# A hybrid decoder step on one Trainium2 core: one more stream step ahead of two transposes, a key multiply in two parts, other mixing rates

## The chip, the core and the metric

The kernel runs on one core of one Trainium2 chip. The metric is the device time of one execution in microseconds (us). The kernel before takes 1997.62 us (median of 3 runs, 1997.28 to 1998.98). A difference of 0.2% is about 4 us.

## The reference, cut to what matters

One layer is computed for a prompt of 1024 tokens and for 8 running sequences of 8 new tokens each (64 "sample" tokens), width 1024, all in float32:

```python
x = x + 0.5 * rms_norm(swiglu(rms_norm(x, norm_ffn1_pre), ffn1_w_gu, ffn1_w_down), norm_ffn1_post)
h = rms_norm(x, norm_mix_pre)
z = h @ w_in + b_in                    # 2816 columns: q, k, v | hq, hf, hi, hg
a = rms_norm(window_attention(q, k, v, attn_sinks), attn_out_norm)   # 8 heads of 64, 2 key heads, window 128
f = lb + (1 - lb) * sigmoid(hf)
o, S = hgrn2_chunked(silu(hq), 1 - f, log(f), hi, s0)                # 4 heads, state 128 x 128
o = rms_norm(o, hg_out_norm) * silu(hg)
x = x + rms_norm(concat([a, o]) @ w_out, norm_mix_post)
x = x + 0.5 * rms_norm(swiglu(rms_norm(x, norm_ffn2_pre), ffn2_w_gu, ffn2_w_down), norm_ffn2_post)
```

Beside the new `x` it returns the last window of keys and values and the recurrent state, for prompt and samples.

## The kernel before

The 1088 tokens are three groups: group 0 has two blocks of 128 prompt tokens and the 64 sample tokens (320 columns), groups 1 and 2 have three blocks of 128 each (384 columns). Every weight matrix is split into a high and a low part (`split`, lines 257 to 259: a cast on ScalarE, then a difference on VectorE), and a product is three matmuls (`mm3`, lines 279 to 281). The rest of the work is fitted between these products.

That is done with streams. A stream is a Python generator with a rate. The code that writes out the big products calls `tick()` at fixed places; each tick adds the rate to a stream's account, and for each whole unit the generator runs to its next `yield`. So a `yield` is a step boundary: what stands behind it is written out at least one step later, with products between. `need(name)` runs a stream to its end at once. What is written out is then ordered engine by engine by a planner that works with its own costs, so the order of the program is that of the ticks only in the large.

The middle of the kernel, the mixing stage (some 690 to 1345 us of the profiled span), goes so: the input projection `w_in_units(0)`, then stream `m0` (the mixer of group 0, rate `RM[0]`) beside the last second-half pieces of the first feed-forward and `w_in_units(1)`; `need("m0")`, then `m1` (rate `RM[1]`) beside `w_out_units(0)`, `w_in_units(2)` and the first columns of the second feed-forward (`f2.head`); `need("m1")`, then `m2` (rate `RM[2]`) beside `w_out_units(1)` and more of `f2.head`; `need("m2")`, then `w_out_units(2)`. Streams `c0`, `c1`, `c2` carry the norms and the transposes between the stages at the same time.

A mixer runs two chains of generators in turn, one step of each (`both`). The attention chain has one `attn_block` for each block: for each of two pairs of heads the scores (`sc`, line 1178), the masked maxima (1186) and exponentials (1195), two yields, the transposes of the probabilities (`pT`, 1206), a yield, the product with the values (`pv`, 1219), a yield; then `finish_attn` (square, `rsqrt`, scale, a yield, the transposes `oT` at 1154, and `put_mix`, which stores the high and the low part). The recurrence chain begins with `intra`: for seven distances `h` of 1 to 64 it multiplies the query half of each block on VectorE (1297) and the key half on GpSimd (1299), between small products (`lv` at 1258; `l32` and `l64` at 1289). Then comes one `hgrn_block` for each block: the key's transposes `kT` (1335), the outputs `av` (1341, 1344), the state's update `u` (1348), and `finish_hgrn` (squares, `rsqrt`, scale at 1314, a yield, the transposes `hT` at 1318, the gate at 1320, `put_mix`). Group 0 also has `sample_attn`, `sample_hgrn` and `kv_out`. The stream of group 1's feed-forward input (`post_n`, `pre_s`: x-loads at line 427, 439, squares at 394, a store to DRAM at 399, in-place scales at 491 and 493, transposes at 511) runs beside `m2`.

Of the kernel before, what the change touches and what calls it, by code (L numbers as in the profile page):

```python
# [14 lines left out]
ALU = mybir.AluOpType  # L15
# [3 lines left out]
P = 128  # L19
# [26 lines left out]
def tile_step(ctx: ExitStack, tc: tile.TileContext, A: dict, O: list):  # L46
    nc = tc.nc
    V, S, G, PE = nc.vector, nc.scalar, nc.gpsimd, nc.tensor
# [8 lines left out]
    def uid(s):  # L57
        cnt[0] += 1
        return f"{s}_{cnt[0]}"
# [4 lines left out]
    def axbank(s="ax"):  # L64
        return ps.tile([P, 512], F32, tag="ax", bufs=4, name=uid(s))
# [31 lines left out]
    def stream(name, gen, rate):  # L97
        streams[name] = [gen, rate, 0.0]
# [155 lines left out]
    def small():  # L254
        return pp.tile([P, 4, 8], F32, tag="small", bufs=10, name=uid("sm"))
# [787 lines left out]
    def mixing(tp, h):  # L1043
        w_in, w_out = A["w_in"][0], A["w_out"][0]

        def t2(shape=(P, 512)):
            return tmp2("t2", shape)
# [90 lines left out]
        def put_mix(n, half, sl, src):  # L1138

            hi, lo = MT[n][0][half], MT[n][1][half]  # L1140
            S.copy(hi[:, :, sl], src)
            V.tensor_tensor(lo[:, :, sl], src, hi[:, :, sl].bitcast(F32), op=ALU.subtract)

        def finish_attn(n, o, r, sl):

            sm = small()
            S.activation(junk[:r], o[:r], AF.Square, accum_out=sm[:r, 0, 0:1])
            V.tensor_scalar(sm[:r, 0, 0:1], sm[:r, 0, 0:1], 1.0 / 512, EPS, op0=ALU.mult, op1=ALU.add)
            rsqrt(sm[:r, 1, 0:1], sm[:r, 0, 0:1], (sm[:r, 2, 0:1], sm[:r, 3, 0:1]))
            V.tensor_scalar(o[:r], o[:r], sm[:r, 1, 0:1], None, op0=ALU.mult)  # L1150
            yield
            b4 = axbank("oT").rearrange("p (c t) -> p c t", c=4)
            for c in range(4):
                PE.transpose(b4[:, c, :r], o[:r, c * P:(c + 1) * P], ident[:r, :r])
            m = t2((P, 4, P))
            V.tensor_tensor(m[:, :, :r], b4[:, :, :r],
                            cols[:, C_AON:C_AON + 4].unsqueeze(2).to_broadcast([P, 4, r]), op=ALU.mult)
            put_mix(n, 0, sl, m[:, :, :r])
            yield
# [70 lines left out]
        def intra(n, res):  # L1230

            z, w, pw = Z[n], WIDTH[n], NPB[n] * P
            K, Q, f = [z[i] for i in ("k", "hq", "f")]
            pool_d = big()
            D = pool_d.rearrange("p a t -> p (a t)")
            At = big(F32, (P, 3, 4, P))
            G.memset(At, 0.0)
            C = tp.tile([P, 3, 4, 32], F32, tag="cm", bufs=1, name=uid("cm"))
            Ds, off = [f[:, :, :w]], 0
            for h in (1, 2, 4, 8, 16, 32, 64):  # L1240
                nx = (w if h <= 4 else pw) // (2 * h)
                Dv = Ds[-1][:, :, :2 * nx].rearrange("p a (x e) -> p a x e", e=2)
                Ds.append(D[:, off:off + 4 * nx].rearrange("p (a x) -> p a x", a=4))
                G.tensor_tensor(Ds[-1], Dv[:, :, :, 0], Dv[:, :, :, 1], op=ALU.mult)
                off += 4 * nx

            def parts(h):

                return [(P, slice(0, 3))] if n else [(P, slice(0, 2))] + ([(NS, slice(2, 3))] if h <= 4 else [])

            def blocks(s, h):
                b5 = axbank(s)[:, :384].rearrange("p (b a t) -> p b a t", b=3, a=4)
                for r, bs in parts(h):
                    for b in range(bs.start, bs.stop):
                        for a in range(4):
                            for i in range(r // 32):
                                cs = slice(b * P + 32 * i, b * P + 32 * i + 32)
                                PE.matmul(b5[32 * i:32 * i + 32, b, a], K[:, a, cs], Q[:, a, cs],  # L1258
                                          start=True, stop=True)
                return b5  # L1260

            b5 = blocks("ld", 1)
            for r, bs in parts(1):
                V.tensor_tensor(C[:r, bs], b5[:r, bs], ident32[:r].unsqueeze(1).unsqueeze(1).to_broadcast(
                    [r, bs.stop - bs.start, 4, 32]), op=ALU.mult)
            V.tensor_tensor(Q[:, :, :w], Q[:, :, :w], f[:, :, :w], op=ALU.mult)
            yield
            for h in reversed(LEVELS):
                if h <= 16:
                    b5 = blocks("lv", h)  # L1270
                    for r, bs in parts(h):
                        nb = 4 * (bs.stop - bs.start)
                        V.copy_predicated(C[:r, bs].rearrange("p b a t -> p (b a) t"),
                                          lmask[h][:r].unsqueeze(1).to_broadcast([r, nb, 32]),
                                          b5[:r, bs].rearrange("p b a t -> p (b a) t"))
                        if (r, h) in ((NS, 4), (P, 16)):
                            for i in range(r // 32):
                                ds = slice(32 * i, 32 * i + 32)
                                G.tensor_copy(At[ds, bs, :, ds], C[ds, bs])
                else:  # L1280
                    per = 3 if h == 32 else 2
                    for b0 in range(0, NPB[n], per):
                        bs = range(b0, min(b0 + per, NPB[n]))
                        b4 = axbank(f"l{h}")[:, :per * 4 * h].rearrange("p (b a t) -> p b a t", b=per, a=4)
                        for b in bs:
                            for a in range(4):
                                for c in range(0, P, 2 * h):
                                    t = b * P + c
                                    PE.matmul(b4[c:c + h, b - b0, a], K[:, a, t:t + h],
                                              Q[:, a, t + h:t + 2 * h], start=True, stop=True)  # L1290
                        for c in range(0, P, 2 * h):
                            S.copy(At[c:c + h, b0:bs[-1] + 1, :, c + h:c + 2 * h], b4[c:c + h, :len(bs)])
                cols = w if h <= 4 else pw
                nx = cols // (2 * h)
                Qv, Kv = [t[:, :, :cols].rearrange("p a (x u) -> p a x u", u=2 * h) for t in (Q, K)]
                Dv = Ds.pop(0)[:, :, :2 * nx].rearrange("p a (x e) -> p a x e", e=2)
                V.tensor_tensor(Qv[:, :, :, h:], Qv[:, :, :, h:], Dv[:, :, :, 0:1].to_broadcast([P, 4, nx, h]),
                                op=ALU.mult)
                G.tensor_tensor(Kv[:, :, :, :h], Kv[:, :, :, :h], Dv[:, :, :, 1:2].to_broadcast([P, 4, nx, h]),
                                op=ALU.mult)  # L1300
                if h == 4:
                    Ds8 = Ds[0]
                yield
            res.update(At=At, Q=Q, K=K, D=Ds[0], D8=Ds8)

        def finish_hgrn(n, bank, r, c0):
            sm = small()
            o = t2((P, 4, P))
            b4 = bank.rearrange("p (a t) -> p a t", a=4)
            for a in range(4):  # L1310
                S.activation(o[:r, a], b4[:r, a], AF.Square, accum_out=sm[:r, 0, a:a + 1])
            V.tensor_scalar(sm[:r, 0, :4], sm[:r, 0, :4], 1.0 / P, EPS, op0=ALU.mult, op1=ALU.add)
            rsqrt(sm[:r, 1, :4], sm[:r, 0, :4], (sm[:r, 2, :4], sm[:r, 3, :4]))
            V.tensor_tensor(o[:r], b4[:r], sm[:r, 1, :4].unsqueeze(2).to_broadcast([r, 4, P]), op=ALU.mult)
            yield
            tb = axbank("hT").rearrange("p (a t) -> p a t", a=4)
            for a in range(4):
                PE.transpose(tb[:, a, :r], o[:r, a], ident[:r, :r])
            m = t2((P, 4, P))
            V.tensor_tensor(m[:, :, :r], tb[:, :, :r], Z[n]["g"][:, :, c0:c0 + r], op=ALU.mult)  # L1320
            put_mix(n, 1, slice(c0, c0 + r), m[:, :, :r])
            yield
# [234 lines left out]
        for g_ in gens:  # L1557
            yield from g_

    RM = [0.95, 1.0, 1.3]  # L1560
    RA0, RA1, RB0, RB1 = 1.2, 0.75, 0.6, 0.8
    HEAD1, HEAD2 = 6, (5, 14, 22)
    PA, PB, PC = (1, 6, 2), (5, 3), (7, 4)
# [8 lines left out]
    xs = [load_x(0, True)]  # L1572
    h = {}
# [65 lines left out]
    with tc.tile_pool(name="mx", bufs=1) as tp:  # L1639
        w_in_units, mixer, w_out_units = mixing(tp, hmix)  # L1640
        need("c0")
        w_in_units(0)
        stream("m0", mixer(0), RM[0])
        half1(1)
# [8 lines left out]
        need("m0")  # L1653
        stream("m1", mixer(1), RM[1])
        w_out_units(0, ym, sums)
# [5 lines left out]
        need("m1")  # L1661
        stream("m2", mixer(2), RM[2])
        w_out_units(1, ym, sums)
# [101 lines left out]
```

## Time and profile before

| | |
|---|---|
| median of 3 runs | 1997.62 us (1997.28 to 1998.98) |
| the profiled execution | 1997.85 us, of which its span is 1996.1 us |
| TensorE matmul busy | 1977.9 us, 99% of the span |
| VectorE, ScalarE, GpSimd busy | 1405.0 us (70%), 942.3 us (47%), 153.1 us (8%) |
| mean granted TensorE clock | 0.995 of full speed |

In the profile PE is TensorE's matmuls, DVE is VectorE, ACT ScalarE, POOL GpSimd, SP the engine that issues most DMAs. A number after L is a line of the kernel. A row of the timeline has start and duration in us, engine, line, operation, output<-input, shape and count, and in brackets the idle time of its engine before it with what ended it. A row of the windows has a stretch in us from the span's start, its length, then for each engine the busy time and the instructions, then PEclk, the granted share of TensorE's clock, then the DMA share and GB/s.

### The profile page before, as it was taken

Reading aid. Unit: us, or ns where it says so; the run is one execution under the profiler, and the core shown is the slowest. Engines: PE = TensorE matmul, PEld = TensorE weight load, DVE = VectorE, ACT = ScalarE, POOL = GpSimd, SP = SyncE. Lnnn points to the kernel's source line nnn. Section 1 sums busy time; section 2 is a strip of 40 time slices with the busy share of each in tenths; the row PEclk is TensorE's granted clock in tenths of the full one; section 3 lists DMA queues with packets and bytes.
Section 4 is the critical chain, followed back from the end, with each engine's and each line's share of the span. In section 5 each row is a group of like instructions: output and inputs, shape, how many; then the busy total and the mean of one; then the engine's idle time right before and its main releaser. Section 6 shows DMA issues by size and latency. Waiting matters only on the chain.

```text
span 1996.1 us, 34286 instructions
## 1 busy us (share of the span) xinstructions
PE 1977.9 (99%) x13331; PEld 1859.0 (93%) x13331; DVE 1405.0 (70%) x2522; ACT 942.3 (47%) x1713; POOL 153.1 (8%) x142
## 2 busy tenths in 40 slices
PE   9999999999999999999999999999999999999998
PEld 9999999999998988779999998989999999999886
DVE  7686767886568656777668656746887887655667
ACT  5753334444445434435344543756544444444452
POOL 0000000000003102210211202000000000000201
PEclk9999999999999999999999999989999999999999
DMA  7735545655777647766334342536565555667874
GB/s 233 221 107 185 189 161 188 227 189 192 234 231 218 183 145 247 233 176 183 108 102 133 95 155 86 171 130 200 165 201 199 191 187 190 211 232 234 287 262 139
DMA packets 377316, 370.28 MB, mean 185 GB/s; under 512 B 40546, under 2 KB 294321, under 8 KB 377137
## 3 DMA queue, kind: packets, MB, share of 16 engines
q1 hardware_dynamic: 371169, 357.21, 56.3%
q10 hardware_dynamic: 5984, 10.88, 1.6%
q8 instruction: 104, 1.70, 0.3%
q14 instruction: 59, 0.48, 0.1%
HBM read 284.31 MB, written 84.71 MB: 185 GB/s over the span
## 4 chain that ended last, share of the span: by engine, by line
PE 96%; DMA 1%; ACT 1%; DVE 1%; issue 0%; POOL 0%; SPq 0%; DVEq 0%; ACTq 0%; POOLq 0%
PE mm L279 28%; PE mm L280 28%; PE mm L281 28%; PE pv L1219 1%; PE sc L1178 1%; PE c L281 1%; PE c L279 1%; PE c L280 1%; DMA raw<-in_ffn_w_gu_dram 1%; PE pT L1206 1%; PE lv L1258 1%; PE tr L511 1%; PE av L1341 0%; PE u L1348 0%; PE av L1344 0%
## 5 line engine op out<-in xcount | busy, mean ns | idle before, releaser
L279 PE MATMUL mm<-h,wsph 128*128 128x320 f32 (+1 forms) x1280 | 406.4, 319 | 0.4 <-ACT sg L676 0.4
L280 PE MATMUL mm<-h,wsph 128*128 128x320 f32 (+1 forms) x1280 | 406.1, 318 | 0.0
L281 PE MATMUL mm<-h,wspl 128*128 128x320 f32 (+1 forms) x1280 | 403.3, 317 | 0.0
L259 DVE TENSOR_TENSOR wspl<-raw,wsph 128x1024 fp32r<-128x1024 f32 x200 | 247.9, 1240 | 151.5 <-ACT wsph L258 145.9
L258 ACT CAST wsph<-raw 128x1024 fp32r<-128x1024 f32 x200 | 209.3, 1048 | 299.1 <-PE mm L280 238.4
L258 ACT CAST w<-raw 128x512 fp32r<-128x512 f32 (+1 forms) x218 | 160.3, 740 | 213.7 <-PE mm L280 113.4
L279 PEld LDWEIGHTS mm<-h,wsph 128*128 128x128 f32 x1280 | 240.7, 188 | 5.5 <-issue 3.8
L259 DVE TENSOR_TENSOR w<-raw,w 128x512 fp32r<-128x512 f32 (+1 forms) x218 | 186.6, 860 | 84.0 <-ACT w L258 83.6
L280 PEld LDWEIGHTS mm<-h,wsph 128*128 128x128 f32 x1280 | 241.0, 188 | 3.1 <-issue 2.7
L281 PEld LDWEIGHTS mm<-h,wspl 128*128 128x128 f32 x1280 | 240.3, 188 | 1.5 <-issue 1.2
L279 PE MATMUL mm<-h,w 128*128 128x384 f32 (+1 forms) x720 | 240.3, 335 | 0.5 <-ACT w L258 0.5
L280 PE MATMUL mm<-h,w 128*128 128x384 f32 (+1 forms) x720 | 240.8, 335 | 0.0
L281 PE MATMUL mm<-h,w 128*128 128x384 f32 (+1 forms) x720 | 235.4, 334 | 0.0
L280 PE MATMUL mm<-w,h 128*128 128x512 f32 x462 | 181.9, 394 | 0.0
L281 PE MATMUL mm<-w,h 128*128 128x512 f32 x462 | 180.3, 392 | 0.0
L279 PE MATMUL mm<-w,h 128*128 128x512 f32 x462 | 180.1, 393 | 0.0
L279 PE MATMUL mm<-big,w 128*128 128x384 f32 x528 | 176.4, 334 | 0.7 <-ACT big L770 0.7
L280 PE MATMUL mm<-big,w 128*128 128x384 f32 x528 | 176.5, 334 | 0.0
L281 PE MATMUL mm<-big,w 128*128 128x384 f32 x528 | 176.2, 334 | 0.0
L279 PEld LDWEIGHTS mm<-h,w 128*128 128x128 f32 x720 | 135.0, 188 | 1.1 <-ACT w L258 0.7
L280 PEld LDWEIGHTS mm<-h,w 128*128 128x128 f32 x720 | 135.2, 188 | 0.1
L281 PEld LDWEIGHTS mm<-h,w 128*128 128x128 f32 x720 | 134.7, 188 | 0.1
(355 smaller groups left out, 3531.3 us busy)
## 6 DMA issues: line engine op xcount, KB each, us to landing
raw<-in_ffn_w_gu_dram SPq DMA_DIRECT2D x156, 512.0 KB
raw<-in_ffn_w_down_dram SPq DMA_DIRECT2D x74, 512.0 KB
raw<-in_w_in_dram SPq DMA_DIRECT2D x54, 512.0 KB
ar<-fa SPq DMA_DIRECT2D x70, 384.0 KB
big<-in_ffn_w_down_dram SPq DMA_DIRECT2D x88, 256.0 KB
fb<-big SPq DMA_DIRECT2D x44, 512.0 KB
fa<-big SPq DMA_DIRECT2D x22, 768.0 KB
raw<-fb SPq DMA_DIRECT2D x30, 512.0 KB
```

The source lines that it names most:

```text
L258: S.copy(hi, src)
L259: (lo_eng or V).tensor_tensor(lo, src, hi.bitcast(F32), op=ALU.subtract)
L279: PE.matmul(out, a[0], b[0], start=first, stop=False, skip_group_check=resume)
L280: PE.matmul(out, a[0], b[1], start=False, stop=False, skip_group_check=resume)
L281: return PE.matmul(out, a[1], b[0], start=False, stop=last, skip_group_check=resume).ins
L511: PE.transpose(bank[:, i * P:(i + 1) * P], y[kh][:, i, k * P:(k + 1) * P], ident)
L1178: PE.matmul(banks[g][:, i * 256:i * 256 + wk], zq[64 * g:64 * g + 64, 2 * pr + i, b * P:(b + 1) * P], kx[64 * g:64 * g + 64, k0:k0 + wk], ...
L1206: PE.transpose(bank[:, (i * nk + kb) * P:(i * nk + kb + 1) * P], pt[g][:, i, kb * P:(kb + 1) * P], ident)
L1219: PE.matmul(ob[:, hd * 64:hd * 64 + 64], pT[g][:, (i * nk + kb) * P:(i * nk + kb + 1) * P], vn[:, vb, g * 64:g * 64 + 64], start=kb == 0, ...
L1258: PE.matmul(b5[32 * i:32 * i + 32, b, a], K[:, a, cs], Q[:, a, cs], start=True, stop=True)
```

## The change

Three edits. (1) `finish_attn` and `finish_hgrn` yield twice, not once, between the scaled result and its transposes. (2) For `h == 64`, GpSimd's multiply of the keys is written as two instructions: the first block, then the other blocks. (3) The rates of the mixers go from 0.95, 1.0, 1.3 to 0.85, 0.95, 1.2.

```diff
@@ finish_attn
             V.tensor_scalar(o[:r], o[:r], sm[:r, 1, 0:1], None, op0=ALU.mult)
+            yield
             yield
             b4 = axbank("oT").rearrange("p (c t) -> p c t", c=4)
@@ intra
-                G.tensor_tensor(Kv[:, :, :, :h], Kv[:, :, :, :h], Dv[:, :, :, 1:2].to_broadcast([P, 4, nx, h]),
-                                op=ALU.mult)
+                for xs in [slice(0, 1), slice(1, nx)] if h == 64 else [slice(0, nx)]:
+                    G.tensor_tensor(Kv[:, :, xs, :h], Kv[:, :, xs, :h],
+                                    Dv[:, :, xs, 1:2].to_broadcast([P, 4, xs.stop - xs.start, h]), op=ALU.mult)
@@ finish_hgrn
             V.tensor_tensor(o[:r], b4[:r], sm[:r, 1, :4].unsqueeze(2).to_broadcast([r, 4, P]), op=ALU.mult)
+            yield
             yield
             tb = axbank("hT").rearrange("p (a t) -> p a t", a=4)
@@
-    RM = [0.95, 1.0, 1.3]
+    RM = [0.85, 0.95, 1.2]
```

## The prediction

> **What bounds the kernel now.** I read the page first, for the engine that has no slack.
>
> ```profile
> span 1996.1 us, 34286 instructions
> ...
> PE 1977.9 (99%) x13331; PEld 1859.0 (93%) x13331; DVE 1405.0 (70%) x2522; ACT 942.3 (47%) x1713; POOL 153.1 (8%) x142
> ```
>
> TensorE is busy for 99% of the span, and the change takes no product away. So it can gain only what TensorE loses: time in which it waits, and time in which it works at a lower clock. The view of waits, for TensorE alone, names the first:
>
> ```profile
> PE pT L1206 <- ACT t L1195: 2.9, 1, 2.9
> PE kT L1335 <- POOL big L1299: 2.4, 1, 2.4
> ...
> PE hT L1318 <- DVE t L1314: 0.9, 1, 0.9
> PE tr L468 <- DVE h L473: 0.9, 1, 0.9
> ...
> PE skT L1379 <- DMA kv<-in_cache_k_win_dram: 0.6, 1, 0.6
> ...
> PE mm L279 <- ACT sg L676: 0.4, 1, 0.4
> ```
>
> All six are in the mixing stage. I then took the stage in stretches of 5 us and kept those in which TensorE is not busy throughout or PEclk is below 1:
>
> ```profile
> 850.00:855.00 5.00, 3.62 (x25) 2.44 (x24) 4.25 (x9) 3.66 (x6) 0.00 (x0) 1.00 0.96 224
> 855.00:860.00 5.00, 4.65 (x22) 3.15 (x22) 2.82 (x5) 1.56 (x2) 0.67 (x1) 1.00 1.21 263
> 1225.00:1230.00 5.00, 2.61 (x34) 2.41 (x34) 2.78 (x3) 0.85 (x2) 2.19 (x1) 1.00 0.38 110
> 1230.00:1235.00 5.00, 5.00 (x29) 5.00 (x28) 2.20 (x11) 4.50 (x12) 0.00 (x0) 0.66 0.00 0
> 1245.00:1250.00 5.00, 4.06 (x31) 3.82 (x30) 3.44 (x13) 3.43 (x11) 0.00 (x0) 1.00 0.35 95
> 1295.00:1300.00 5.00, 2.10 (x12) 1.40 (x10) 1.94 (x5) 4.28 (x10) 0.00 (x0) 0.86 0.54 140
> 1300.00:1305.00 5.00, 5.00 (x19) 3.67 (x17) 1.10 (x2) 4.27 (x9) 0.00 (x0) 0.50 0.19 73
> 1305.00:1310.00 5.00, 5.00 (x16) 3.85 (x16) 1.56 (x8) 0.36 (x1) 0.00 (x0) 0.50 0.10 35
> 1310.00:1315.00 5.00, 5.00 (x32) 4.91 (x31) 1.39 (x6) 2.75 (x10) 0.00 (x0) 0.77 0.00 0
> 1325.00:1330.00 5.00, 4.61 (x33) 4.34 (x32) 1.92 (x2) 2.13 (x5) 0.00 (x0) 1.00 0.65 195
> sum 50.00, PE 41.66 PEld 34.98 DVE 23.39 ACT 27.80 POOL 2.86; mean PE 4.17 PEld 3.50 DVE 2.34 ACT 2.78 POOL 0.29
> ```
>
> Two columns matter. Idle: 50.00 - 41.66 = 8.34 us. Clock: (1 - 0.66) x 5 = 1.70 us behind the wait that ends at 1229.65, and (0.14 + 0.50 + 0.50 + 0.23) x 5 = 6.85 us behind the one that ends at 1298.70; together 8.55 us. After the shorter gaps (1.38, 0.94, 0.39 us) the clock stays at 1.00. So the two long waits cost more than their idle time, and the whole stake is 8.34 + 8.55 = 16.9 us: the lowest the change can reach is 1997.85 - 16.9 = 1981.0.
>
> The Trainium skill ("TensorE: Matmul & The Clock Gate", section "Part 1: The HAM clock gate") says that the clock goes to one half after an idle window of about 3.4 us. The trace has the half, but after gaps of 2.4 and 2.9 us.
>
> **The key multiply in two parts.** The timeline around the second longest wait (group 2's first key transposes):
>
> ```profile
> 1225.65 1.61 PE L1289 MATMUL l<-big,big 128*64 128x64 f32 x24
> 1226.83 0.85 ACT L1292 COPY big<-l 64x512 f32<-64x512 f32 x2 [1.86 <-PE l L1289]
> 1227.30 0.96 DVE L1297 TENSOR_TENSOR big<-big,big 128x768 f32<-128x768 f32 x1 [1.07 <-PE l L1289]
> 1227.41 2.19 POOL L1299 TENSOR_TENSOR big<-big,big 128x768 f32<-128x768 f32 x1 [3.05 <-PE l L1289]
> 1229.65 0.55 PE L1335 MATMUL kT<-ident,big 128*128 128x128 f32 x3 [2.39 <-POOL big L1299]
> ```
>
> GpSimd starts after the last of the 24 records of `l64` and takes 2.19 us with no product between. In the changed program's order the first part waits for block 0's products only (the first 8 of 24 records), and `kT` waits for the first part only. So 16/24 x 1.61 = 1.07 us of `l64` run beside it. The part has a third of the elements: 2.19 / 3 = 0.73 us if time goes by elements (upper bound: no less than this row, 2.19). Ready at 1227.26 - 1.07 + 0.15 + 0.73 = 1227.07, before `l64` ends at 1227.26. What is late next is `av`, behind `kT`: it needs VectorE's query multiply, whose end is 1227.30 + 0.96 = 1228.26, while 4 transposes cover some 0.5 us from 1227.3. That leaves 0.5 us (bounds 0 and 1.3), and a gap this short has cost no clock here: 2.39 + 1.70 - 0.5 = 3.6 us gained. GpSimd issues three instructions more in all; it is 8% busy.
>
> **The last long wait.** VectorE's last maximum, and ScalarE's queue just ahead of the wait:
>
> ```profile
> 1295.41 0.16 DVE L1191 TENSOR_SCALAR sm<-sm 128x4 f32<-128x4 f32 x1
> ```
> ```profile
> 1295.69 1.04 ACT L258 CAST wsph<-raw 128x1024 fp32r<-128x1024 f32 x1 [2.47 <-PE mm L280]
> 1296.75 1.28 ACT L1195 ACT_TABLE_LOAD   x1
> 1298.04 0.51 ACT L1195 ACTIVATE t<-t,sm 128x256 f32<-128x256 f32 x1
> ```
>
> The inputs were there at 1295.57, but in ScalarE's queue a weight cast stands ahead, which itself waits until TensorE has left the buffer; 1.04 + 1.28 + 0.51 = 2.83 us follow with TensorE idle. Cover is products, and one product of 320 columns takes:
>
> ```profile
> 1233.99 0.30 PE L279 MATMUL mm<-h,wsph 128*128 128x320 f32 x1
> 1237.21 0.31 PE L280 MATMUL mm<-h,wsph 128*128 128x320 f32 x1
> ```
>
> 22 steps lie between these two rows: 3.22 / 22 = 0.146 us. In the order view 48 products stand between these scores and their `pT` before, 63 after: 15 x 0.146 = 2.2 us more; and one weight cast, not two, stands between the probabilities' maxima and the exponentials, which takes out the 1.04 us and its wait. 2.2 + 1.04 is over 2.9, so I take the wait as gone, with its 6.85 us of clock: 9.75 us. If the cover fell short by the cast, 1 us would stay.
>
> **The extra step before the transposes.** It delays each `oT` and `hT` and the stores behind them; no DMA is in the step. In group 2's first block 46 products stand between `u` and `hT` before, 60 after: 14 x 0.146 = 2.0 us against a wait of 0.94, gone. The 0.39 us at 1329 (`sg` behind the last attention work) goes too. At 850 to 858 us four transposes of `c1` (L468) and `skT` stood back to back; with the slower `m0` the order view has them in pairs with products between: 1.38 + 0.35 = 1.73 us, taken as gone (bounds 0 and 1.73). Sum of the gains: 3.6 + 9.75 + 0.94 + 0.39 + 1.73 = 16.4.
>
> **What the rates add.** Slower mixers end later and meet other work. Steps: `m2` has 57 and an end, at 1.2 a tick 48.3 of the 52 ticks up to `need("m2")` (before: 52 at 1.3, 40); `m0` 73 and an end, at 0.85 87.1 of 92 (before: 71.6). Nothing is drained, and 3.7 ticks of 12 products each (6.5 us) remain for `m2`. The DMAs that move with `m0` are the sample state, the cached keys and values, and sixteen small reads, which hold SP's queue, where weight loads stand too:
>
> ```profile
> 928.39 5.54 SPq L1430 DMA_DIRECT2D t<-osc  x15
> ```
>
> They go from beside the feed-forward into `w_in_units(1)`; the weights are loaded ahead, so I take 0 (bounds 0 and 0.6, the `skT` wait above; at worst 5.5).
>
> The new meeting is in `m2`: the exponentials of the second block now come behind all six squares of `c1`:
>
> ```profile
> 1254.05 0.63 ACT L394 ACTIVATE junk<-big 128x512 bf16<-128x512 f32 x1 [0.25 <-DVE big L439]
> ```
>
> In the changed order, between those scores and their first exponential, ScalarE has 6 squares (3.8 us), 3 weight casts (3.1), a table load (1.28) and some four small copies (4 x 0.51, the exponential's row, 2.0): with the exponential 10.7 us, against 94 products, 13.8 us. The squares wait for VectorE's six L439 and the casts for TensorE, so the 3 us of slack need not hold. Bounds 0 and 2.9 (the wait just treated); I take 1.5, the middle. Behind them an in-place scale (L491) waits for the store to DRAM issued right after the exponentials, and the copy that `pv` needs stands behind that; I put 0.7 on it, with the wait for one cached load, 0.62, as the nearest row. So 2.2 us come back: the net gain is 16.4 - 2.2 = 14.2, and 1997.85 - 14.2 = 1983.7, which against the median (0.23 us lower) I round to 1984.
>
> Five more table loads are in the changed program (26 for 21): 5 x 1.28 = 6.4 us on an engine that is 47% busy; one is in the sum above, the others are covered. The Trainium skill ("ScalarE: Activation LUTs", section "What ACT_TABLE_LOAD costs") gives 1.28 us and 1.38 us of drain for each; here the exponential starts 0.01 us after the load's end, so the row decides, and by the page the second block's wait would be 1.4 us longer.
>
> **The rivals.**
> - The new meeting is as long as the old (2.9 us) and takes the clock down once: idle 0.5 + 2.9 + 0.7 = 4.1, clock 1.70 to 6.85. Gain 16.9 - 4.1 - (1.70 to 6.85) = 11.1 to 5.9: 1986.8 to 1991.9. For it: the same queue, the same weight casts. Against: almost twice the products between. Chance 0.22.
> - The clock does not fall from gaps of 2 to 3 us but from something else in these stretches (transposes and small products), and the half speed stays: gain 8.34 - 2.7 = 5.6, 1992.2. PEclk falling right behind just the two longest gaps speaks against. Chance 0.05. The Trainium skill's window of 3.4 us ("TensorE: Matmul & The Clock Gate", the section above) would speak for it.
> - The edits do not do what they say: the planner's order meets the same waits elsewhere, 1997.9, within 2 us. Chance 0.08.
> - Slower: the mixers end too late, and the output projection stands still for the last stored result. If each of the three ends waits like the worst wait, with its clock: 3 x (2.9 + 6.85) = 29.3 against the 14.2 gained, 2013. It decides where the last `put_mix` lands after the 3.7 ticks that `m2` has left. Against it: in the changed order `oT`, then two to three us of TensorE work, stand before the first product that needs it. Chance 0.07.
>
> **How the numbers follow.** The forecast, waits as summed, has chance 0.58; its own range is 1981.0 (every wait gone) to 1987. The range over the cases goes to the upper end of the first rival, just past the second: 1981 to 1992.5. What the measurement can tell from no change is 0.2%, 4 us: faster is 0.58 + 0.22 + 0.05 = 0.85, same 0.08, slower 0.07.
>
> **What would show it.** In the profile after: no `kT` wait on L1299 over 0.6 us; no `pT` wait in the third block; PEclk at 1.00 from 1210 to 1345; one new wait of 1 to 2 us of `pT` on L1195's successor in the second block of group 2, and a short one of `pv`. It is wrong if PEclk falls again in the mixing stage, or if a product of the output projection waits for `put_mix`.

## The result and the profile after

The changed kernel takes 1979.19 us (median of 4 runs, 1977.18 to 1979.89); the kernel before takes 1998.30 us beside it. The ratio is 0.9903 with a 95% interval of 0.9886 to 0.9920: 19.1 us faster, 16.0 to 22.8. The forecast was 14 us, its range ended at 1981.0, and that end was given as the lowest the change could reach. So more was gained than the prediction had found to be lost. The interval of the gain reaches down to 16.0 us, below the 16.9 of that floor, so it is the rows below, more than the time, that show what the prediction left out.

The profiled execution of the changed kernel took 1979.89 us. Its page, for TensorE:

```profile
span 1978.2 us, 34310 instructions
...
PE 1965.7 (99%) x13331; PEld 1850.8 (94%) x13331; DVE 1406.3 (71%) x2522; ACT 948.6 (48%) x1718; POOL 154.6 (8%) x145
```

The span is 17.9 us shorter. Busy time fell by 1977.9 - 1965.7 = 12.2 us with the same 13331 products, idle time by the other 5.7. The prediction knew only one way for busy time to fall, the clock (8.55 us at most). That is the first sign that something else moved. The waits of TensorE in the changed kernel:

```profile
PE av L1347 <- DVE big L1298: 1.2, 1, 1.2
PE ax L566 <- DVE sm L570: 1.1, 1, 1.1
PE mm L280 <- DVE h L1142: 1.0, 1, 1.0
...
PE tr L598 <- DMA big<-in_x_sample_dram: 0.5, 1, 0.5
```

All six of the old waits in the mixing stage (`pT`, `kT`, `hT`, `tr`, `skT`, `sg`) are gone. Two are new there: `av` behind VectorE's query multiply, and the first product of the output projection behind `put_mix` (L1142). The stretches of 5 us of the mixing stage in which TensorE is not busy throughout, or the clock is below 1, were ten; now they are four:

```profile
915.00:920.00 5.00, 5.00 (x17) 0.87 0.41 111
920.00:925.00 5.00, 5.00 (x31) 0.79 0.38 110
970.00:975.00 5.00, 3.97 (x36) 1.00 0.37 105
1225.00:1230.00 5.00, 3.81 (x43) 1.00 0.61 148
```

Idle time is 1.03 + 1.19 = 2.22 us (before 8.34), the clock's loss (0.13 + 0.21) x 5 = 1.70 (before 8.55). Both together explain 6.1 + 6.85 = 13.0 us of the stage, in these two profiled executions. What is left shows in the groups by line, of before and then of the changed kernel (busy time and mean ns behind the bar):

```profile
L1178 PE MATMUL sc<-kx,big 64*128 64x256 f32 (+1 forms) x128 | 27.1, 406 | 0.0
...
L1469 PE MATMUL su<-t,t 32*128 32x512 f32 x16 | 6.7, 640 | 0.0
```
```profile
L1179 PE MATMUL sc<-kx,big 64*128 64x256 f32 (+1 forms) x128 | 19.6, 389 | 0.0
...
L1472 PE MATMUL su<-t,t 32*128 32x512 f32 x16 | 7.9, 640 | 0.0
```

The same 128 records of the scores are busy for 7.5 us less, though one record takes as long as before (389 ns; the 406 has eight records at half speed in it). The timeline says how. Before, at the scores of one pair of heads:

```profile
1030.51 1.13 PE L1178 MATMUL sc<-kx,big 64*128 64x256 f32 x4
...
1033.69 1.13 PE L1178 MATMUL sc<-kx,big 64*128 64x256 f32 x4
```

and the same scores in the changed kernel:

```profile
1041.33 1.13 PE L1179 MATMUL sc<-kx,big 64*128 64x256 f32 x8
```

Eight records take the time of four. The scores of two heads use the two 64-row halves of the array (`zq[64 * g:64 * g + 64]`), and issued in turn the halves work side by side; issued apart, with other products between, each half takes the whole 1.06 us from its start to the next product's. Of the sixteen score groups, seven stand apart before and two after. Five groups x 1.06 = 5.3 us; the other 2 of the 7.5 us are two halves that ran at half speed in before, and are counted under the clock. The Trainium skill ("TensorE: Matmul & The Clock Gate", section "Part 3: Packing small matmuls — row/col tiling") says that products on different row groups overlap almost whole; the two rows agree, 1.13 us for four and for eight.

The samples' state update `su` goes the other way: three of four pairs stand apart after, two before, 1.1 us lost. 6.1 + 6.85 + 5.3 - 1.1 = 17.2 us; the stage as a whole is 18.3 us shorter by its products' starts, and 1.1 us of that I have not assigned.

### The profile page after: what moved, and what is told of

Same layout as the page of the kernel before. It is cut to its first block, busy times and chain, and to the rows that moved or that the text cites. A ratio compares the mean times of both kernels' runs of the same rounds, so it can differ in the third digit from the quotient of the medians.

```text
span 1978.2 us, 34310 instructions
## 1 busy us (share of the span) xinstructions
PE 1965.7 (99%) x13331; PEld 1850.8 (94%) x13331; DVE 1406.3 (71%) x2522; ACT 948.6 (48%) x1718; POOL 154.6 (8%) x145
## 4 chain that ended last, share of the span: by engine, by line
PE 96%; DMA 1%; DVE 1%; SPq 0%; ACT 0%; issue 0%; DVEq 0%; ACTq 0%
PE mm L279 28%; PE mm L281 28%; PE mm L280 28%; PE pv L1220 1%; PE c L279 1%; PE c L281 1%; PE c L280 1%; DMA raw<-in_ffn_w_gu_dram 1%; PE sc L1179 1%; PE lv L1259 1%; PE pT L1207 1%; PE tr L511 1%; PE su L1472 0%; PE u L1351 0%; PE av L1344 0%; DMA big<-in_ffn_w_down_dram 0%
```

## The experiments

Theory P is that kept-together score groups are worth 1.06 us each, beside the waits and the clock; theory W that only waits and clock count. In what follows, idle time is 655 us less TensorE's busy time from 690 to 1345 us, and gains are against the kernel before on the same chip (1997.58 us for the first four kernels, 1998.33 for the next four, 1999.27 for the last).

**Scores tied together, nothing else changed.**

```diff
+                PE.matmul(banks[0][:, :1], ident, ones[:, :1], start=True, stop=True)
                 for i in range(2):
-                    for g in range(2):
+                    for g in range(1, -1, -1):
+                        with tc.issue_after(lead.ins) if (i, g) != (0, 1) else nullcontext():
...
```

> The kernel before with one thing added: a one-column product claims the second score bank first, and the four score products of a pair of heads are tied together in the order, so that the two 64-row halves are never issued apart (before, seven of the sixteen score groups stand as two separate halves, 1.06 us each, where a whole group takes 1.08 us). Rates, steps and the key multiply are as before. Theory P (kept-together scores are worth about 1.07 us each): 7 x 1.07 = 7.5 us faster, less 16 small claiming products of at most 0.11 us, 1.8: 5.7 to 7.5 faster, near 1991, if the old waits stay where they are. Theory W (the gain is only in waits and clock, the score halves don't count): no change, 1998 within 1 us, or slower by the 1.8.

It took 1989.62 us, ratio 0.9962 (0.9948 to 0.9977): 8.0 us faster, just past theory P's 7.5. The total alone does not put theory W out, because waits and clock changed too; the rows do:

```profile
L1180 PE MATMUL sc<-kx,big 64*128 64x256 f32 (+1 forms) x128 | 17.3, 389 | 0.0
...
L1176 PE MATMUL sc<-ones,ident 128*128 128x1 f32 x32 | 4.9, 223 | 0.0
```
```profile
690.00:1345.00 655.00, 643.46 (x5599) 1.00 0.51 153
```

The scores fell by 9.8 us (7.4 by the seven groups, most of the rest because no half falls into half speed now). The claims, the one-column products, are busy for 4.9 us where 1.8 was allowed, and idle time rose from 8.3 to 11.5 us, against a loss to the clock that fell from 8.55 to 1.7: waits and clock together are 3.6 us of the gain. So the price per group is confirmed by the rows; that the total came out as forecast is luck.

**Each edit alone.** The three kernels are before with one of the edits of the change's diff.

> Only the key multiply in two parts. Theory of the prediction: the wait of kT on GpSimd (2.39 us) goes, a wait of av of 0.5 to 1.2 us takes its place, and with it the first half-speed stretch (1.70 us of loss): 2.9 to 3.6 us faster, 1995, the other waits as before. Rival: another wait of the same length stands there, and the time is the same, 1998.

The division alone: 1995.66 us, 0.9990 (0.9980 to 0.9999), 1.9 faster. The `kT` wait and its half speed are gone, as both the trace and theory had it, but idle time in the stage is 655 - 646.36 = 8.6 us, as much as before (in an execution 2.1 us above the median): the order shifts, and new or longer waits of 0.6 to 1.0 us come at `hT`, `oT` and two of the big products.

> Only the extra step ahead of both kinds of transposes. Four score groups stand apart in its order, where before has seven. Theory P: 3 x 1.07 = 3.2 us from that; the hT wait (0.94) gone; the last long pT wait and its 6.85 us of clock are only touched as far as the exponentials move: 36 to 39 products of 320 columns between the last scores and their pT where before had 48, so it may even stay. 1994 if it stays, 1984 if it goes. Theory W without P: 0.94 only, 1997.4, or 1987.6 if the long wait goes.

The steps alone: 1984.25 us, 0.9934 (0.9917 to 0.9951), 13.3 faster, the bulk of the change. Waits left in its stage:

```profile
PE kT L1337 <- POOL big L1300: 2.4, 1, 2.4
...
PE pT L1207 <- ACT t L1196: 0.9, 2, 0.5
PE pv L1220 <- DVE t L1210: 0.6, 1, 0.6
```

The last long `pT` wait is down to 0.5 us, with only 27 products of 320 columns between these scores and their `pT` (my 36 to 39 belonged to another block), where before has 48 and waits 2.9. So here it is not the cover that grew, it is the chain that became shorter. In before, a 1.75 us difference (L501, of the feed-forward's input) and a weight difference of 1.22 us stood among the maxima on VectorE, another weight difference just ahead of them, and the cast ahead of the exponentials had itself waited 2.47 us for TensorE. In the steps-only kernel, ScalarE's queue ahead of the exponentials:

```profile
1294.05 1.05 ACT L258 CAST wsph<-raw 128x1024 fp32r<-128x1024 f32 x1 [0.54 <-PE mm L280]
...
1295.99 0.58 ACT L516 ACTIVATE big<-tr,cols 128x384 f32<-128x384 f32 x1 [0.89 <-PE tr L511]
1296.59 1.28 ACT L1196 ACT_TABLE_LOAD   x1
1297.88 0.51 ACT L1196 ACTIVATE t<-t,sm 128x256 f32<-128x256 f32 x1
```

The cast is over before the last maximum is there (VectorE ends it at 1297.02), and only the table load stands in the way. From the scores to the first exponential it is 5.5 us here, and was 10.7 in before.

> Only the three rates. Six score groups stand apart (before seven). Theory of the prediction: the rates spread the pieces, the waits at 850 to 858 us (1.73) go and the last pT wait with its clock (9.75): 11.5 us, and 1.07 for the one score group, 1985.8; the kT wait (2.39 and 1.70 of clock) stays. Rival: the last wait needs the extra steps as well, and stays: 1995.

The rates alone: 1993.57 us, 0.9979 (0.9969 to 0.9988), 4.0 faster, between the two forecasts, and neither foresaw what happened:

```profile
PE oT L1154 <- DVE t L1150: 3.6, 1, 3.6
PE kT L1335 <- POOL big L1299: 2.4, 1, 2.4
```

The long `pT` wait is gone here too, as the first forecast had it, but the last mixer ends at the very start of the last output projection, `oT` makes TensorE wait for 3.6 us, and the clock goes to one half again. This is the slow rival's mechanism, once and with its clock.

**The changed kernel without one edit.**

> The changed kernel with the old rates (0.95, 1.0, 1.3): extra steps and divided key multiply only. Four score groups stand apart, as with the steps alone. If the parts add up: the steps alone gave 13.3 us, the division alone 1.9, so 15.2 us against before, 1982.4; the kT wait of 2.4 us with its half-speed stretch (1.7) is gone from the steps-only kernel, and a wait of av of 0.2 to 1.2 comes. Rival (the rates carry the rest of the gain, through the two more score groups that stay whole, 2.1 us, and nothing else): 1981.3.

Without the rates: 1981.87 us, 0.9918 (0.9904 to 0.9933), 16.5 faster. The interval of that gain, 13.4 to 19.2 us, holds both the sum of the two parts (15.2) and the rival's 16 to 17, so this run does not tell them apart. Four score groups apart, scores 21.8 us busy, idle 655 - 651.43 = 3.6 us, no half speed in the stage of this execution. By the ratios the rates add some 3 us to the other two edits, but the two intervals overlap.

> The changed kernel with the key multiply in one instruction. Three score groups stand apart (changed: two). kT waits 2.4 us again in place of av's 1.2: 1.2 us slower than the changed kernel, 1.07 for the score group, and 1.7 more if the 2.4 us lie within one of the windows of 3.41 us that the clock goes by, nothing if they straddle two: 2.3 or 4.0 us slower, 1981.5 or 1983.2. Rival (the division alone gave 1.9 only): 1981.1 with no kT wait over 2.

Without the division: 1982.24 us, 0.9919 (0.9902 to 0.9936), 16.1 faster. `kT` waits 2.4 us again, and in the profiled execution the clock stays at 1.00, as foreseen for a gap across two windows (below). But that execution took 1979.44 us at a granted clock of 0.999; the other three took 1982.1 to 1982.5 at 0.997 to 0.998, so what the trace shows of the clock does not hold for the median. By the ratios this kernel is some 3 us slower than the changed one, between the 2.3 and the 4.0 that were foreseen without and with half speed.

> The changed kernel without the extra step ahead of hT (the one ahead of oT stays). No score group stands apart (changed: two), and two su halves more do (four single pairs for three). Theory P: 2.1 us faster from the scores, 1.05 slower from su. But only 20 products stand between the last block's scores and its transposes (changed: 31 to 68), 2.9 us against a chain of maxima, exponentials and a table load: a pT wait of 1 to 3 us. Net 0 to 2 us slower than the changed kernel, 1979 to 1981; 1984 if a window goes to half speed. Theory W (score halves don't count): 1 to 3 us slower by the wait alone, plus clock.

Without the step ahead of `hT`: 1985.59 us, 0.9937 (0.9922 to 0.9951), 12.7 faster. All score groups stand whole (17.8 us busy), and yet it is 6 us or more slower than the changed kernel:

```profile
1295.59 1.28 ACT L1196 ACT_TABLE_LOAD   x1
1297.69 0.51 ACT L1196 ACTIVATE t<-t,sm 128x256 f32<-128x256 f32 x1 [0.82 <-DVE sm L1192]
```
```profile
PE pT L1207 <- ACT t L1196: 4.3, 2, 3.4
PE hT L1320 <- DVE t L1316: 1.2, 1, 1.2
```

Between the third block's first scores and their `pT` this order has no product of 320 columns at all (the 20 of my expectation belong to its second pair), so nothing covers maxima, table load and exponential, and one window goes to half speed. Whole scores alone don't make the kernel fast; waits and clock weigh as much.

> The changed kernel without the extra step ahead of oT (the one ahead of hT stays). Four score groups stand apart (changed: two), two su pairs (changed: three). Theory P alone: 2.1 slower by the scores, 1.05 faster by su: 1980.2 if no wait comes back. If the step ahead of oT is what frees the scores' and transposes' banks in time, a wait of oT or pT of 1 to 4 us returns: 1981 to 1985 with or without a window at half speed.

Without the step ahead of `oT`: 1983.37 us, 0.9923 (0.9910 to 0.9935), 15.9 faster, some 4 us slower than the changed kernel: 2.2 of it from two more score groups apart (21.8 us) and 3.6 from waits of 0.3 to 1.2 us (idle 655 - 649.17 = 5.8), less 1.2 from a `su` pair more that stands whole; each of the two traces has 1.7 us of half speed.

**Further than the change.** The samples' pairs tied:

```diff
+                ubs = [axbank("su").rearrange("p (b t) -> p b t", b=4) for _ in range(2)]
+                PE.matmul(ubs[0][:1, 0, :1], ident[:1, :1], ones[:1, :1], start=True, stop=True)
+                lead = PE.matmul(ubs[1], kn[sr[1], a], vb[sr[1]], start=True, stop=True)
+                with tc.issue_after(lead.ins):
+                    PE.matmul(ubs[0], kn[sr[0], a], vb[sr[0]], start=True, stop=True)
...
```

> The changed kernel with the two products of each su pair (the state update of the samples) tied together as the scores were in the first experiment, with a one-element claiming product for each of the four pairs. In the changed kernel three pairs stand as separate halves; 3.41 us of half speed begin right behind two such pairs, without any idle time ahead. Theory A (the clock goes by how little TensorE does in a window, idle or not): with the halves side by side the window is fuller and the half speed at 918 us goes: 1.7 us, and two pairs x 1.05 = 2.1 us, less 4 claims of at most 0.14: 3.2 us faster, 1976. Theory I (only idle time takes the clock down, and this stretch has another cause): 1.5 to 2.1 faster from the pairs, the half-speed stretch stays.

1975.73 us, 0.9886 (0.9871 to 0.9900), some 3.4 us faster than the changed kernel, and the half speed is gone from the trace, which is in line with theory A. But the trace of the kernel without the division has the same two `su` pairs apart in one window and no half speed, so theory A is not shown, and what took the clock down at 918 us stays open.

Then the two last score groups tied as well:

```diff
+                tied = (n, b, pr) in ((0, 1, 1), (2, 2, 0))
+                if tied:
+                    PE.matmul(banks[0][:1, :1], ident[:1, :1], ones[:1, :1], start=True, stop=True)
...
```

> The kernel with tied su pairs (1975.7), and the two score groups that still stand apart tied as well, each with a one-element claiming product. Theory P: 2 x 1.07 less 2 claims of 0.12 to 0.27 each: 1.6 to 1.9 faster, 1974.0, all else as it was; the score rows together fall from 18.30 to 16.2 us. Theory W: no change, 1975.7.

1974.64 us, 0.9877 (0.9863 to 0.9890). The kernel before it ran on another chip: the medians differ by 1.1 us, the ratios by 1.8, and their intervals overlap. The scores fell as foreseen, and the claims are small now,

```profile
L1183 PE MATMUL sc<-kx,big 64*128 64x256 f32 (+1 forms) x128 | 17.3, 389 | 0.0
...
L1179 PE MATMUL sc<-ones,ident 1*1 1x1 f32 x4 | 0.4, 159 | 0.0
```

from 19.6 us: 2.3 us for two groups. In the traces idle time grew from 2.7 to 3.6 us, most of it at `spv` (0.5 to 1.2), which takes a part of it back.

Then VectorE's multiply divided:

```diff
-                V.tensor_tensor(Qv[:, :, :, h:], Qv[:, :, :, h:], Dv[:, :, :, 0:1].to_broadcast([P, 4, nx, h]),
-                                op=ALU.mult)
+                for xs in [slice(0, 1), slice(1, nx)] if h == 64 else [slice(0, nx)]:
+                    V.tensor_tensor(Qv[:, :, xs, h:], Qv[:, :, xs, h:],
+                                    Dv[:, :, xs, 0:1].to_broadcast([P, 4, xs.stop - xs.start, h]), op=ALU.mult)
```

> The kernel before this one in the list, and VectorE's query multiply at distance 64 in two parts as well, the first block first. The av wait of 1.19 us behind it should fall to 0 to 0.5, since the part for the first block has a third of the elements of an instruction of 0.96 us: 0.7 to 1.2 faster, 1973. Rival: the wait of the first projection product behind (big from the output projection) takes its place, as in the kernel with the division alone (0.7): 0 to 0.5 faster.

1973.03 us, 0.9869 (0.9856 to 0.9883): 1.6 less than the kernel before it on the same chip, the `av` wait gone. This kernel beats both, before by 26 us and the changed one by 6 to 7.

Last, the first mixer's rate raised (`RM = [0.88, 0.95, 1.2]`):

> The kernel before this one in the list with the first mixer's rate 0.88 in place of 0.85. The first mixer ends some 3 ticks earlier (74 steps at 0.88 are 84.1 ticks, at 0.85 87.1), so that its last stored result lies 36 products, about 6 us, further ahead of the output projection's first product, and that product's wait of 1.02 us on it goes: 1 us faster. Rival: the samples' pieces meet the second feed-forward piece differently, and a wait of 0.5 to 2 us comes at 850 to 910 us instead: 0 to 1 slower.

1982.28 us, 9 us slower, which neither theory had. The rival's waits came (`su` 0.8 us at 851 us, with 3.41 us of half speed behind it, and `spT` 1.7 us at 912), but the larger part lies at the end of the first mixer. The profiled execution took 1985.16 us, 2.9 above the median, so its rows add up to more than 9 us. On TensorE:

```profile
955.83 0.32 PE L1426 MATMUL spv<-kv,t 128*32 128x64 f32 x8
956.08 0.31 PE L1430 MATMUL spv<-vnew,t 8*32 8x64 f32 x8
...
972.66 0.68 PE L1155 MATMUL oT<-ident,t 64*128 64x64 f32 x4 [5.83 <-issue]
```

on SP, then on VectorE and ScalarE:

```profile
946.43 9.83 SPq L265 DMA_DIRECT2D raw<-in_w_out_dram  x3
956.35 0.43 SPq L1439 DMA_DIRECT2D t<-osc  x1
956.84 0.34 SPq L1434 DMA_DIRECT2D osc<-t  x1
957.23 6.30 SPq L1439 DMA_DIRECT2D t<-osc  x15
```
```profile
956.47 0.29 DVE L1433 TENSOR_SCALAR t<-spv,sm 128x64 f32<-128x64 f32 x1 [0.60 <-PE spv L1430]
```
```profile
964.98 0.63 ACT L1147 ACTIVATE junk<-t 64x512 bf16<-64x512 f32 x1 [1.35 <-DMA t<-osc]
```

The last piece of the samples' attention (`spv`) comes off VectorE at 956.76, its store is issued at 956.84, and fifteen of the sixteen reads stand behind that store. The three weight loads ahead of it in the queue are issued by 956.26, so they kept back only the first read. The norm starts on what was read at 964.98, and its last scale on VectorE ends at 972.56, 7.6 us later, with other groups' work between its steps (in the kernel with 0.85 the same takes 3.4 us). `oT`, which stands ahead of the output projection, makes TensorE wait 5.8 us, with half speed behind. What differs is the cover: with 0.85 96 products of the projections stand between the last `spv` and this `oT`, with 0.88 only 59. At some 0.17 us each the 37 that are missing are 6.4 us, an estimate from the rows of this trace. Why the higher rate brought the last `spv` so near to the projection is not shown. So 0.03 in one rate costs half of what the whole change gained.

## Why the prediction missed, point by point

- **The stake (16.9 us, floor 1981.0): this step failed.** It took TensorE's busy time at full clock as fixed, and so put the score rows at nothing: seven groups in halves hold 7 x 1.06 = 7.4 us. The rows `x4` were there in the trace of before. With 5.3 us of them gained and 1.1 lost on `su`, the floor did not hold.
- **The key multiply (3.6 us): right in mechanism, 0.7 too high.** `kT` comes right after the first part, as forecast, and `av` is late next, but by 1.19 us, not 0.5 (within the bounds of 0 and 1.3). The mis-sized term is VectorE's multiply: 0.96 us in the trace of before, 1.85 here, since GpSimd's second part runs beside it:

```profile
1225.68 0.62 POOL L1301 TENSOR_TENSOR big<-big,big 128x256 f32<-128x256 f32 x1 [2.11 <-PE l L1290]
...
1226.40 0.66 PE L1338 MATMUL kT<-ident,big 128*128 128x128 f32 x4
1226.55 1.05 POOL L1301 TENSOR_TENSOR big<-big,big 128x512 f32<-128x512 f32 x1 [0.25 <-PE l L1290]
1226.56 1.85 DVE L1298 TENSOR_TENSOR big<-big,big 128x768 f32<-128x768 f32 x1 [1.13 <-PE l L1290]
...
1228.47 0.49 PE L1347 MATMUL av<-st,big 128*128 128x128 f32 x2 [1.19 <-DVE big L1298]
```

  The Trainium skill ("SBUF — State Buffer", section "Summary: rules for kernel authors") says that of two such operations (VectorE's with two inputs in SBUF, GpSimd's reading SBUF) the second to start stands still until the first is done. The trace agrees: VectorE starts 0.01 us behind GpSimd and takes 0.9 us longer, near GpSimd's 1.05. In before GpSimd was the second, with 2.19 us. The kernel with the division alone has the two instructions the other way round: VectorE starts at 1228.71 and takes 0.96 us, GpSimd's second part starts at 1228.75 and takes 1.82, and `av` waits only 0.2. So in the changed kernel the second part, which starts just ahead of VectorE's multiply, holds it up, and `av` with it.
- **The last long `pT` wait (9.75 us): gone, as forecast**, with its clock. In the changed kernel the reason given holds: 63 products stand between. But it is not the only way: the steps alone get nearly there with 27, by a shorter chain ahead of the exponentials.
- **`hT`, `sg`, `tr` and `skT` (3.1 us): gone.**
- **The new meeting (2.2 us back): it did not come.** In the changed kernel no `pT` and no `pv` wait is over the view's threshold. In the steps-only kernel, with fewer products between, it is there: 0.38 and 0.62 us. The cover of 94 products held, and I should have taken the bound of zero.
- **The rates at nothing: wrong by 1.0 to 2.7 us.** The projection's first product waits 1.0 us for `put_mix`, the slow rival's place; the kernel with the old rates has no such wait. And 1.7 us are lost to the clock at 918 us; whether the rates brought that is open, as is its cause. I had written that either would make the prediction wrong; both came and the kernel is faster than forecast, because the score rows outweigh them.
- **The sum:** 14.2 - 0.7 + 2.2 - 1.0 - 1.7 + 5.3 - 1.1 = 17.2, and 1.1 unassigned, make the 18.3 us of the stage. In the forecast's own sum, 1983.65 less the 0.23 us is 1983.4, which does not round to 1984; nothing hangs on it.

What put the scores back together is argued, not shown: four banks serve all the small products, a group needs two, and when one comes free alone the planner issues half. That claiming the second bank first keeps every group whole is in line with it. It is not shown either which edit parts or joins which group: the steps alone leave four apart, the rates alone six, the changed kernel two.

## What to carry to other kernels

Where TensorE is 99% busy, ask of the busy time too whether it could be less: products on separate rows of the array are cheap only when they are issued in turn, and any change of order may part or join them. Compare counts and durations by group, `x4` against `x8`, before calling a sum of waits a floor. A small change of a rate may gain on one wait and lose several times that at the next deadline; count the products that are left between a mixer's last pieces and the product that needs them. A trace is one execution: see where its time lies among the others of the kernel before its clock is taken for that of the median.

## What the runs showed of the hardware that I had not expected

The half-speed stretches lie on a fixed grid. In before they begin at 1230.37 and at 1298.63, 68.26 us or 20 x 3.413 apart, and last 3.41 and 13.65, 1 and 4 x 3.413. So a wait's length alone does not say what it costs in clock; where it falls on the grid counts too. The windows with the `kT` wait of 2.4 us, in before:

```profile
1226.96:1230.37 3.41, 1.02 (x13) 1.00 0.53 156
1230.37:1233.78 3.41, 3.41 (x18) 0.50 0.00 0
```

and with the scores tied, where the grid cuts the same wait in two:

```profile
1226.74:1230.16 3.42, 1.68 (x26) 1.00 0.43 127
1230.16:1233.57 3.41, 2.45 (x20) 1.00 0.09 26
```

The first is followed by half speed, the second is not. Against the start of the span the grid lies elsewhere in each trace: 1230.37 us in before, 1224.35 with the steps alone and 918.67 in the changed kernel leave 1.6, 2.4 and 0.5 us after whole windows of 3.413. So the same wait may fall into one window in one execution and into two in the next. The Trainium skill ("TensorE: Matmul & The Clock Gate", section "Part 1: The HAM clock gate") calls the window free-running, 4096 cycles or 3413 ns; the traces agree. Busy time alone does not decide: with the steps alone a window with 1.47 us busy led to half speed,

```profile
1220.94:1224.35 3.41, 1.47 (x24) 1.00 0.50 146
1224.35:1227.76 3.41, 2.91 (x14) 0.50 0.20 48
```

without the division one with 1.47 did not,

```profile
1224.40:1227.81 3.41, 1.47 (x13) 1.00 0.89 285
1227.81:1231.22 3.41, 3.41 (x29) 1.00 0.30 87
```

and in the changed kernel a window that was busy throughout did:

```profile
915.26:918.67 3.41, 3.41 (x11) 1.00 0.38 74
918.67:922.09 3.42, 3.42 (x14) 0.51 0.75 240
```

Of that window 2.1 us are `su`, which uses 32 of 128 rows. Without the step ahead of `oT`, a window with 2.71 us busy (1311.10 to 1314.51) was followed by half speed too. Where the line runs, no run here shows.
